# Mamba input products of the first pass in plain float32

## The chip, the cores and the metric

The kernel runs on one core of one Trainium2 chip. The metric is the device time of one execution in microseconds (us), the median over runs; lower is better. The core has a matrix engine (PE, with its weight loads shown apart as PEld), a vector engine (DVE), an activation engine (ACT), GpSimd (POOL), and a queue engine (SP) that here only issues transfers. ACT and POOL issue transfers too. Each engine works through its own list of instructions in order.

## The reference

One layer of a streaming encoder for 512 prompt rows and 8 streams of 16 rows, width 1024, all in float32. What matters here is the front of the layer: the rows are normalized and modulated to `h`, and `h @ w_in` gives ten products. Those of the Mamba branch are `z` (2048 columns) and `xbc` (3072 columns); `xbc` goes through a causal convolution of four taps and a SiLU before the state space scan, and `z` gates the scan's result.

```
h = (_rms(x) * norm1_w * (1.0 + sc1) + sh1).astype(x.dtype)
proj = h @ w_in
q_r, f_r, i_r, g_r, z, xbc, dt_r, ga_r, gb_r = jnp.split(proj, cuts, axis=-1)
...
xc = conv_b + xp[:, 0:t] * conv_w[0]
for j in range(1, SSM_CONV):
    xc = xc + xp[:, j:j + t] * conv_w[j]
xc = jax.nn.silu(xc.astype(f32))
...
y = y.reshape(bn, t, SSM_D_INNER) * jax.nn.silu(z.astype(f32))
```

After the token mixer come the merge of the branches, a product-key lookup and the experts. Results and the final states must agree with a float32 computation.

## The kernel before

The 640 rows are worked on in two passes, with the rows along the free dimension and the features on partitions: pass A (`p`, 256 rows: the first 128 of the prompt and the 128 of the streams) and pass B (`q`, the other 384 rows of the prompt). `run` (line 331) sets the stages in this order: the first modulation of both passes (`first_mod`, line 543); the HGRN inputs of both passes with pass A's HGRN heads (`hgrn_in`, 572); pass A's Mamba (`mamba_in`, 806); pass A's merge and product keys; pass B's HGRN and Mamba with expert rows gathered beside them; pass B's merge and keys; the experts. The kernel is written with a tile framework that orders each engine's instructions itself, by a simulated timeline and with the written order as priority, and adds the waits. So products may stand on PE ahead of work that is written earlier, but every engine's list is fixed when the kernel is built.

A weight block is 1024 x 128 (512 KB), eight chunks of 128 x 128. There are two ways to multiply with it:

- Split (`wsplit` 255, `mm3` 265): SP loads the block to a `raw` buffer (five in this stage); ACT rounds it to `whi` (float32r, line 261) and DVE forms the rest `wlo` (line 253); four buffers of each. The activations lie in SBUF in two parts also, `p.H` (`hhA`, `hlA`). PE then makes three float32r matmuls for each chunk (whi by hlA, whi by hhA, wlo by hhA), 24 for a block, all at line 273. The `raw` buffer is free once DVE has read it.
- Plain (`proj32` 282): SP loads `raw`, and PE multiplies it as float32 with float32 activations, one matmul for each chunk, which the profile shows as two MATMUL records (line 289), so 16 records for a block. The `raw` buffer is free when PE has read it.

`mproj` (292) takes the plain way where the pass has `h32`, the activations kept in float32. Before the change only pass B has it: `first_mod` stores its modulated rows to the DRAM tile `hf_d`, and `run` loads them back after pass A's Mamba (lines 403 and 404).

In `mamba_in`, `mamba_out` (833) runs for four groups. Each takes six convolution products and four z products through `mproj`, so 40 blocks in all; `conv` (772) reads a product from its PSUM bank (ACT `xp`, line 784; DVE `xs`, line 793), and `zproj` (842) by a SiLU on ACT. `mamba_group` (853) then does the scan with float32 matmuls, a chain over ACT, DVE and PE. Between groups stand the 16 gate products (`gate` 827, through `projs` 295), four of them ahead of the first group. Products go to four PSUM banks, `pj`. The tiles of this stage lie in the pools `gtA`, `mcA` and `mpA`, which open where the HGRN pool `gpA` has closed; a new tile waits for those old tiles whose bytes it takes.

Of the kernel before, what the change touches and what calls it, by code (L numbers as in the profile page):

```python
# [8 lines left out]
F32 = mybir.dt.float32  # L9
# [8 lines left out]
P = 128  # L18
D = 1024
KD = D // P  # L20
# [170 lines left out]
class Kernel:  # L191
# [100 lines left out]
    def mproj(self, p, src):  # L292
        return self.proj(src, p.H) if p.h32 is None else self.proj32(src, p.h32)

    def projs(self, src, passes):

        if passes[0].h32 is not None:
            return [self.proj32(src, p.h32) for p in passes]
        w = self.wsplit(src)
        out = []  # L300
        for p in passes:
            ps = self.pj()
            self.mm3(ps, w, P, p.H)
            out.append(ps[:, :p.W])
        self.step()
        return out
# [24 lines left out]
    def run(self):  # L331
        nc, I, V, A, ctx = self.nc, self.I, self.V, self.A, self.ctx
# [28 lines left out]
        p, q = Pass("A", I["xA"], (0, None), 0), Pass("B", I["xB"], (1, 2, 3), 2 * P)  # L361
# [14 lines left out]
        self.wp = hw.enter_context(self.pool("wp"))  # L376
        for t in (p, q):
            t.H = [self.ha.tile([P, KD, t.W], F32R, name="h" + c + t.name) for c in "hl"]
        self.hf_d = self.dram.tile([KD, P, q.W], F32, name="hf_d")
        with self.pool("x1") as xp:  # L380
            self.ada_in(xp)
            ada = self.ada(0)
# [17 lines left out]
        self.nraw, self.nhl = NRAW, NHL  # L400
        bw = ExitStack()
        q.h32 = hb.enter_context(self.pool("hb")).tile([P, KD, q.W], F32, name="h32")
        for j in range(0, KD, 4):
            nc.sync.dma_start(q.h32[:, j:j + 4, :], self.hf_d[j:j + 4].rearrange("m p w -> p m w"))
        self.sr = ctx.enter_context(self.pool("sr", side="right"))
        ah = ExitStack()
        self.rw = ah.enter_context(self.pool("rw", side="right"))
# [3 lines left out]
        sp = bw.enter_context(self.pool("stg"))  # L411
# [131 lines left out]
    def first_mod(self, p, xp):  # L543
        hh, hl = p.H
        for k in range(KD):
            t1 = p.xn[:, k, :]
            self.modulate(p, t1, None, None, self.a1, 0, k)
            if not p.sample:
                self.nc.sync.dma_start(self.hf_d[k], t1)
            self.A.activation(hh[:, k, :], t1, AF.Copy)  # L550
            self.lo(hl[:, k, :], t1, hh[:, k, :])

# [253 lines left out]
    def mamba_in(self, md):  # L806
        nc, I, O, (p, q) = self.nc, self.I, self.O, self.passes
        with self.pool("gtA") as sp:
            p.hist, q.hist = md.tile([P, 24, 8, 3], F32, name="hist"), None
            nc.scalar.dma_start(p.hist, I["hist"])  # L810
            p.cnv, q.cnv = md.tile([P, 24, 8, 3], F32, name="cnvA"), self.md.tile([P, 24, 1, 3], F32, name="cnvB")
            gates = list(range(16))

            def more(n):
                for _ in range(min(n, len(gates))):
                    j = gates.pop(0)
                    self.gate(self.passes if j < GS else self.passes[:1], sp, j)

            more(GA)
            with self.pool("mcA") as p.mc, self.pool("mpA") as mp:  # L820
                for g in range(4):
                    self.mamba_out(p, mp, mp, g)
                    more(GG)
                more(16)
            nc.scalar.dma_start(O["conv_s"], p.cnv)
# [581 lines left out]
```

## Time and profile before

| | |
|---|---|
| median of 3 runs | 2906.17 us (2903.67 to 2910.95) |
| the profiled execution's own time | 2904.54 us |
| its span, first to last instruction | 2902.7 us |
| PE busy | 2697.5 us, 93% of the span |
| DVE busy | 2132.2 us, 73% |
| ACT busy | 1344.4 us, 46% |
| mean granted PE clock | 0.966 of full speed |

Busy time is a union of the records on an engine. A matmul's record is longer than the distance to the next one, because matmuls overlap in the array; what a run of them costs is read from the distance of their starts. "Idle before" a row is time in which the engine had nothing running, with the instruction that ended it. Times within the span are counted from its first instruction.

### The profile page before, as it was taken

The numbers are of one execution on the slowest core, as the hardware profiler recorded it, in microseconds if no ns is written. First come the engines' busy times: TensorE is split into PE (matmuls) and PEld (weight loads), VectorE is DVE, ScalarE is ACT, GpSimd is POOL, SyncE is SP. The second block draws the span as 40 slices with busy tenths as digits, with TensorE's granted clock in tenths as the row PEclk, the third lists the DMA queues.
The fourth block names the chain that finished last, engine by engine and source line by source line (L and its number), as shares of the span: only waits on it lengthen the run. The fifth ranks groups of instructions, "written<-read, shape, count | busy, mean of one in ns | idle before, by whom it ended". The sixth has DMA issues, their size and how long they took to land. (4 is left out here: it accounts for less than half of the span.)

```text
span 2902.7 us, 41739 instructions
## 1 busy us (share of the span) xinstructions
PE 2697.5 (93%) x15177; PEld 2258.9 (78%) x15177; DVE 2132.2 (73%) x4364; ACT 1344.4 (46%) x2056; POOL 731.8 (25%) x682
## 2 busy tenths in 40 slices
PE   6999989998989999977898998997999999999998
PEld 3988868777877555645897777896878999999997
DVE  4556748777778778776788897775667777777776
ACT  3667647764532355644334244554333333333334
POOL 0000002000000443331353476300124444333330
PEclk8999989999999999988998999998999999999999
DMA  8344456657534787666798698967889888888984
GB/s 298 122 150 157 141 181 213 211 175 269 186 115 128 259 293 267 240 218 222 288 330 329 235 338 324 329 224 275 273 285 324 302 313 299 306 302 308 306 303 155
DMA packets 274150, 725.14 MB, mean 250 GB/s; under 512 B 25456, under 2 KB 112760, under 8 KB 270488
## 3 DMA queue, kind: packets, MB, share of 16 engines
q1 hardware_dynamic: 153144, 348.50, 35.7%
q0 software_dynamic: 73920, 269.66, 26.5%
q10 hardware_dynamic: 46880, 104.32, 9.9%
q8 instruction: 119, 1.95, 0.3%
q14 instruction: 87, 0.71, 0.1%
HBM read 646.36 MB, written 76.02 MB: 249 GB/s over the span
## 5 line engine op out<-in xcount | busy, mean ns | idle before, releaser
L1195 POOL DMA_INDIRECT row<-in_u,eidx x256 | 336.5, 1315 | 973.8 <-DVE row L1200 519.8
L1200 DVE SCALAR_TENSOR_TENSOR row<-row,h2t 128x1024 f32<-128x1024 f32 x256 | 307.6, 1220 | 48.1 <-DMA row<-in_u,eidx 47.7
L1294 PE MATMUL po<-vl,wh 128*128 128x512 f32 x768 | 301.0, 392 | 18.8 <-ACT wh L1348 15.2
L289 PE MATMUL pj<-h,raw 128*128 128x384 f32 x896 | 305.2, 495 | 3.2 <-ACT xpB L784 2.3
L1294 PE MATMUL po<-vh,wh 128*128 128x512 f32 x768 | 301.6, 393 | 0.0
L1294 PE MATMUL po<-vh,wl 128*128 128x512 f32 x768 | 299.8, 391 | 0.0
L261 ACT ACTIVATE whi<-raw 128x1024 fp32r<-128x1024 f32 (+1 forms) x169 | 176.5, 1049 | 222.2 <-PE pj L273 135.8
L289 PEld LDWEIGHTS pj<-h,raw 128*128 128x128 f32 x896 | 170.0, 194 | 116.5 <-issue 8.1
L253 DVE TENSOR_TENSOR wlo<-raw,whi 128x1024 fp32r<-128x1024 f32 (+1 forms) x169 | 204.9, 1215 | 63.7 <-ACT whi L261 62.2
L1256 ACT ACTIVATE uh<-ur 128x1024 fp32r<-128x1024 f32 x128 | 135.8, 1061 | 241.9 <-PE s L1264 228.0
L253 DVE TENSOR_TENSOR ul<-ur,uh 128x1024 fp32r<-128x1024 f32 x128 | 156.5, 1222 | 98.7 <-ACT uh L1256 98.5
L1264 PE MATMUL s<-h2h,ul 128*128 128x384 f32 x672 | 225.6, 336 | 0.0
L1264 PE MATMUL s<-h2l,uh 128*128 128x384 f32 x672 | 225.4, 335 | 0.0
L1264 PE MATMUL s<-h2h,uh 128*128 128x384 f32 x672 | 225.1, 335 | 0.0
L1195 POOL DMA_INDIRECT row<-in_v,eidx x128 | 151.2, 1182 | 277.7 <-DVE acc L1210 253.4
L273 PE MATMUL pj<-hlA,whi 128*128 128x256 f32 x648 | 194.0, 299 | 11.2 <-ACT stGA L830 4.9
L273 PE MATMUL pj<-hhA,wlo 128*128 128x256 f32 x648 | 191.4, 295 | 1.6 <-DVE wlo L253 1.6
L273 PE MATMUL pj<-hhA,whi 128*128 128x256 f32 x648 | 191.2, 295 | 0.0
L1294 PEld LDWEIGHTS po<-vl,wh 128*128 128x128 f32 x768 | 145.0, 189 | 49.9 <-ACT wh L1348 15.4
L253 DVE TENSOR_TENSOR vl<-vr,vh 128x1024 fp32r<-128x1024 f32 x128 | 158.5, 1240 | 22.5 <-ACT vh L1306 22.5
L1306 ACT ACTIVATE vh<-vr 128x1024 fp32r<-128x1024 f32 x128 | 135.0, 1056 | 83.7 <-PE po L1294 83.2
L1294 PEld LDWEIGHTS po<-vh,wl 128*128 128x128 f32 x768 | 144.1, 188 | 30.3
(482 smaller groups left out, 7005.6 us busy)
## 6 DMA issues: line engine op xcount, KB each, us to landing
raw<-in_w_in SPq DMA_DIRECT2D x136, 512.0 KB, 4.4
ur<-in_uT SPq DMA_DIRECT2D x128, 512.0 KB, 6.5
vr<-in_vP SPq DMA_DIRECT2D x128, 512.0 KB, 5.8
raw<-in_w_ada SPq DMA_DIRECT2D x48, 512.0 KB, 5.2
g_d<-gt ACTq DMA_DIRECT2D x24, 1024.0 KB, 6.7
gm<-g_d SPq DMA_DIRECT2D x48, 512.0 KB, 7.1
raw<-in_w_b SPq DMA_DIRECT2D x32, 512.0 KB, 5.7
raw<-in_w_q SPq DMA_DIRECT2D x32, 512.0 KB, 4.7
```

The source lines that it names most:

```text
L253: self.V.tensor_tensor(out, raw, hi.bitcast(F32), OP.subtract)
L261: self.A.activation(hi[:, :n], raw[:, :n], AF.Copy)
L273: self.PE.matmul(ps[:m, :W], a[:, k * m:(k + 1) * m], b[:, k0 + k, :], start=start and q == 0, stop=stop and q == 3 * nk - 1)
L289: self.PE.matmul(ps[:, :W], raw[:, k * P:(k + 1) * P], x[:, k, :], start=k == 0, stop=k == KD - 1)
L1195: self.paced(self.G.indirect_dma_start(out=r, out_offset=None, in_=src, in_offset=bass.IndirectOffsetOnAxis(ap=at, axis=0)), pin)
L1200: self.paced(V.scalar_tensor_tensor(r, r, 1.0, self.h2t[:, n, :], OP.mult, OP.mult, accum_out=act[:, s:s + 1]), pin)
L1256: A.activation(uh, ur, AF.Copy)
L1264: PE.matmul(ps[:, :W], a[:, k, :], c[:, k, :], start=q == 0, stop=q == 3 * KD - 1)
L1294: PE.matmul(po[n][hf], a[:, ts], c[:, ds], start=b == 0 and q == 0, stop=b == P - 1 and q == 2)
L1306: A.activation(vh, vr, AF.Copy)
```

## The change

Pass A takes the plain way for its 40 Mamba products too. `first_mod` stores the modulated rows of both passes to DRAM (eight further transfers of 128 KB on SP's queue); `mamba_in` makes a tile `h32` of 8 KB per partition for pass A in `gtA` and loads it with two transfers of 512 KB from SP, written ahead of the first gates. Since `p.h32` is then set, `mproj` takes `proj32` for the convolution and z products, and their weight blocks are no longer split. The gates go through `projs`, whose condition now excludes pass A, so they stay split and `p.H` stays in use.

```diff
+    def h_in(self, p):
+        for j in range(0, KD, 4):
+            self.nc.sync.dma_start(p.h32[:, j:j + 4, :], p.hf_d[j:j + 4].rearrange("m p w -> p m w"))
+
     def projs(self, src, passes):
 
-        if passes[0].h32 is not None:
+        if not passes[0].sample and passes[0].h32 is not None:
             return [self.proj32(src, p.h32) for p in passes]
...
-        self.hf_d = self.dram.tile([KD, P, q.W], F32, name="hf_d")
+        for t in (p, q):
+            t.hf_d = self.dram.tile([KD, P, t.W], F32, name="hf_d" + t.name)
...
-        for j in range(0, KD, 4):
-            nc.sync.dma_start(q.h32[:, j:j + 4, :], self.hf_d[j:j + 4].rearrange("m p w -> p m w"))
+        self.h_in(q)
...
-            if not p.sample:
-                self.nc.sync.dma_start(self.hf_d[k], t1)
+            self.nc.sync.dma_start(p.hf_d[k], t1)
...
+            p.h32 = sp.tile([P, KD, p.W], F32, name="h32", bufs=1)
+            self.h_in(p)
             gates = list(range(16))
```

## Rows read from the trace of the kernel before

**Rows 1.** The page's first part: the busy time of each engine, its share of the span, and its instructions.
```profile
PE 2697.5 (93%) x15177; PEld 2258.9 (78%) x15177; DVE 2132.2 (73%) x4364; ACT 1344.4 (46%) x2056; POOL 731.8 (25%) x682
```

**Rows 2.** The view by stretches: start and end, length, then busy time and records of PE, PEld, DVE, ACT and POOL, mean granted PE clock, DMA share, GB/s. The four stretches are the HGRN inputs, the end of pass A's HGRN, pass A's Mamba up to the last gate product, and the crossing to the merge.
```profile
64.00:366.00 302.00, 301.30 (x2062) 270.00 (x2061) 177.84 (x486) 199.69 (x302) 0.00 (x0) 0.99 0.43 145
366.00:423.40 57.40, 44.29 (x254) 32.60 (x252) 29.41 (x95) 25.07 (x40) 0.64 (x6) 0.83 0.50 167
423.40:657.20 233.80, 217.95 (x1573) 187.76 (x1574) 176.64 (x392) 164.95 (x304) 32.99 (x106) 0.97 0.62 200
657.20:700.00 42.80, 33.82 (x189) 25.55 (x188) 29.78 (x63) 22.18 (x43) 0.00 (x0) 0.88 0.94 335
```

**Rows 3.** The groups of instructions of the stretch from 423.4 to 657.2 us: line, engine, operation, tiles, count, then busy us and mean ns of one, then idle time before and what ended it.
```profile
L273 PE MATMUL pj<-hlA,whi 128*128 128x256 f32 x416 | 126.1, 303 | 11.2 <-ACT stGA L830 4.9 <-DVE xs L793 3.1 <-ACT whi L261 2.2
L273 PE MATMUL pj<-hhA,wlo 128*128 128x256 f32 x416 | 124.2, 298 | 1.6 <-DVE wlo L253 1.6
...
L253 DVE TENSOR_TENSOR wlo<-raw,whi 128x1024 fp32r<-128x1024 f32 x48 | 58.7, 1222 | 13.1 <-ACT whi L261 11.7 <-DMA H<-in_s_ssm 0.7 <-DMA out_ssm_s<-H 0.6
L261 ACT ACTIVATE whi<-raw 128x1024 fp32r<-128x1024 f32 x48 | 50.4, 1052 | 37.6 <-PE pj L273 21.9 <-DMA h_c<-Hs 10.5 <-DMA out_ssm_s<-H 3.4
```

**Rows 4.** PE's timeline in that stage, first and last of a run of 30 split matmuls that nothing interrupts: start, length, line, tiles.
```profile
597.02 0.28 PE L273 MATMUL pj<-hhA,whi 128*128 128x256 f32 x1
...
600.48 0.28 PE L273 MATMUL pj<-hlA,whi 128*128 128x256 f32 x1
```

**Rows 5.** PE's timeline in pass A's product keys, where `proj32` works on the same 256 rows: two whole blocks of 16 records, each with the instruction that follows it.
```profile
822.66 3.62 PE L289 MATMUL pj<-h2f,raw 128*128 128x256 f32 x16
826.12 0.83 PE L672 MATMUL sm<-vh,khat 128*128 128x128 f32 x6
...
831.14 3.62 PE L289 MATMUL pj<-h2f,raw 128*128 128x256 f32 x16
834.60 0.81 PE L319 MATMUL sm<-osq,ones 128*128 128x384 f32 x2
```

**Rows 6.** PE's timeline in pass B, a half block of `proj32` on 384 rows between other float32 matmuls.
```profile
1204.53 2.75 PE L289 MATMUL pj<-h,raw 128*128 128x384 f32 x8
1207.11 0.83 PE L649 MATMUL sm<-lvc 128*128 128x128 f32 x6
```

**Rows 7.** What PE waited for from 423.4 to 657.2 us, longest in total first: who waited, for whom, us in total, times, longest.
```profile
PE sm L327 <- ACT btok L863: 6.0, 2, 3.4
PE pj L273 <- ACT stGA L830: 4.9, 1, 4.9
PE pj L273 <- DVE xs L793: 3.1, 2, 2.3
PE pj L273 <- ACT whi L261: 2.2, 2, 1.1
PE pj L273 <- DVE wlo L253: 1.6, 2, 0.9
PE sm L327 <- DVE cbm L870: 1.0, 1, 1.0
PE sm L319 <- ACT xTg L960: 1.0, 1, 1.0
PE pj L273 <- ACT zt L843: 0.9, 1, 0.9
```

**Rows 8.** PE's timeline at the crossing from HGRN to Mamba: its first product after the wait, and the next.
```profile
423.37 0.58 PE L273 MATMUL pj<-hlA,whi 128*128 128x256 f32 x1 [4.90 <-ACT stGA L830]
423.75 0.41 PE L273 MATMUL pj<-hhA,whi 128*128 128x256 f32 x1
```

**Rows 9.** POOL's timeline there: its first work on a tile of the new pools, with its idle time and what ended it.
```profile
414.61 0.10 POOL L781 MEMSET xpA<- 128x3 f32 x1 [412.04 <-PE sm L690]
```

**Rows 10.** DVE's timeline there: the last instruction of pass A's HGRN.
```profile
420.82 0.42 DVE L708 TENSOR_TENSOR oTA<-oTA,kqA 128x256 f32<-128x256 f32 x1
```

**Rows 11.** DMA throughput from 400 to 445 us in 40 slices of 1.125 us.
```profile
GB/s 222 415 433 408 387 87 4 0 0 0 58 0 0 0 0 0 0 102 189 361 388 353 209 137 117 169 240 388 253 368 257 322 382 233 291 182 106 0 182 366
```

**Rows 12.** DMA issues from 423 to 657 us: tile and source, queue, count, size of one, median us from issue to landing.
```profile
raw<-in_w_in SPq DMA_DIRECT2D x43, 512.0 KB, 4.1
```

**Rows 13.** SP's timeline around the first modulation: start, time for the issues, tile and source, count.
```profile
42.31 0.33 SPq L260 DMA_DIRECT2D raw<-in_w_in  x1
47.51 2.25 SPq L549 DMA_DIRECT2D hf_d<-xB  x4
49.87 0.38 SPq L492 DMA_DIRECT2D raw<-in_w_ada  x1
50.34 2.10 SPq L549 DMA_DIRECT2D hf_d<-xB  x4
```

**Rows 14.** PE's timeline there: the matmuls that wait for that transfer of `w_ada`.
```profile
54.46 1.92 PE L495 MATMUL ad<-raw,cs 128*32 128x512 f32 x4 [3.59 <-DMA raw<-in_w_ada]
```

**Rows 15.** The stores of line 549 (pass B's eight): shortest, median and longest issue in ns, first and last start.
```profile
L549 SPq DMA_DIRECT2D hf_d<-xB x8: 320/416/702, 47.5 to 52.1; - x8
```

## The prediction

> **What bounds the kernel now.** I read the page's first part, then the view by stretches, then in the stage that the change touches its groups, PE's timeline and PE's waits. The first part says that PE is busy 93% of the span and DVE 73% [rows 1]. An average doesn't tell what one stage is worth, so the stage is read alone: pass A's Mamba, from PE's first product after HGRN to its last gate product, is 233.8 us long. PE is busy in 217.95 of them, DVE in 176.64 (76%), ACT in 164.95 (71%) [rows 2]. PE is idle for 15.85 us, and its granted clock is 0.97. Its waits in order of size are for the evacuation of group inputs (ACT `btok`, 6.0), for a free PSUM bank at the very start (4.9, ended by ACT's gate), and for banks that DVE or ACT still reads (`xs` 3.1, `zt` 0.9); for a split weight it waits 2.2 + 1.6 = 3.8 us only [rows 7]. So PE's own work sets the length, and the split on ACT and DVE lies beside it almost entirely. The reader is to see that the change takes work from the two engines that have room and puts some on the one that has none.
>
> A busy PE could still be hollow, since matmul records overlap. The starts settle that: 30 split matmuls with nothing between them start 3.46 us apart from first to last, 0.1193 us each, where each record is 0.28 long [rows 4].
>
> **The change part by part.** *The products.* A split block is 24 matmuls of 0.1193 = 2.863 us [rows 4]. For a plain block on the same 256 rows the trace has the very operation, in the product keys: 16 records, and from their start to the start of what follows 3.46 us, twice over (826.12 - 822.66, 834.60 - 831.14) [rows 5]. Pass B, at 384 rows, agrees: half a block takes 2.58 us, 0.3225 a record, 1.49 times the 0.216 of 256 rows [rows 6]. So a block costs PE 3.46 - 2.863 = 0.60 us more, and 40 blocks 23.9 us. The 12 gates of this stage stay split: 1248 records of line 273 are 52 blocks [rows 3], of which 40 change.
>
> The page "FP8 and Floating Point Precision" of the Trainium skill (section "TensorE Precision Notes") counts true float32 as four passes through the array. Taken against three passes of the split, a plain block would cost 4/3 of 2.863 = 3.82 us, and 40 blocks 38 us. The rows disagree with that ratio: 3.46 / 2.863 is 1.21, because the split's short matmuls don't reach the rate of one pass, so I don't use it in the sum.
>
> *The splits.* 40 times 1.052 us on ACT and 1.222 on DVE go [rows 3], 42 and 49 us in all; four of each lie before 423.4, so 38 and 44 us leave this stage. They are beside PE's work. What they give back is what PE waited for: the 3.8 us for weights, most of which can vanish; and part of the 4.0 us for `xs` and `zt`, where a read of a bank can stand behind a split on DVE or ACT [rows 7]. The 6.0 for `btok` is a chain (product, convolution, SiLU, transpose, copy) that gets a little shorter. Bounds: nothing, and all 15.85 us of idle [rows 2] with the 0.03 of the clock in 233.8 us, 7.0 us more. I take 6 us: 3 of the weights, 2 of the banks, 1 of the chain.
>
> *The buffers.* A `raw` buffer is now held until PE has read it, not until DVE has. Five buffers at 3.46 us make 17.3 us for one turn, against 4.1 us from issue to landing [rows 12]. I cost that at nothing; with bursts of state transfers a landing would have to grow past 13 us to show.
>
> *The load of `h32`.* It is written on SP's queue ahead of the gates' weights, and every weight block stands behind it if the order keeps that. Its bytes were HGRN's. The first touch of a new tile that the trace shows follows a matmul of the last HGRN head, at 414.61 [rows 9]; HGRN's last instruction ends at 420.82 + 0.42 = 421.24 [rows 10]. So the two transfers start between 414.6 and 421.3. DMA is nearly idle from about 407 to 419 us and full from 421 on [rows 11]. With a transfer like the weights', 4.1 us [rows 12], and a second one behind it at some 400 GB/s (1.3 us), `h32` is there between 420.0 and 426.7, later still if it shares with the states' loads. PE's first product starts at 423.37, because a gate must first free a bank [rows 8]. Hence 0 to 3.3 us of new wait, and 2 more with sharing and a PE clock that comes back late: after today's wait the matmul at 423.75 is 0.41 long [rows 8], where the same one takes 0.28 in the steady run [rows 4]. I take 1 us, near the lower end, since `h32` is the first tile of the new pool and the closed pool's first tiles are HGRN's values (`vsb`), which a matmul of line 690 reads last.
>
> *The stores.* Eight more, at 0.416 us each on SP [rows 15]. Pass B's stand from 47.51 to 52.4, and SP issued nothing from 42.64 to 47.51 [rows 13], so pass A's first can fall into that gap. What is queued behind them is the transfer of `w_ada` issued at 49.87; PE waits for it until 54.46 [rows 14] and has no slack afterwards, as the HGRN stretch is PE-bound without a gap (301.30 of 302.00) [rows 2]. Bounds 0 and 8 x 0.416 = 3.3 us; I take 1, as some four of eight come before it and part of those fall into the gap. The reverse, a gain, is excluded: nothing is taken from that queue.
>
> *Afterwards.* The crossing to the merge waits on the scan's tail and on transfers, with PE busy 33.82 of 42.80 [rows 2]; its instructions don't change. Everything after pass A's Mamba moves as a whole. The order on all engines is made anew, which can move any stage by a few us either way; I give that 5 us in the range and nothing in the sum.
>
> **Sum:** 23.9 - 6 + 1 + 1 = +19.9 us. On the profiled execution (2904.54, of which 2902.7 are span) that is 2924.4; the median of the runs lies 1.6 above that execution, so 2926.
>
> **The rivals.**
>
> *1. The freed engines pay for it (not slower).* With ACT and DVE down to 54% and 57% of its old length, (165 - 38) / 234 and (177 - 44) / 234, no wait is left and the clock stays up: 15.85 + 7.0 = 22.9 us come back against 25.9 (23.9 + 2 of transfers). That gives +3, 2909. It speaks for it that more filler on PE hides chains; against it that only 3.8 us of the waits name a split, and that the 4.9 at the start and the first gates have nothing to do with one. It decides in favour of "no change" once more than 17 us come back.
>
> *2. Faster.* The end of pass A's HGRN has 13.1 us of idle PE and a clock of 0.83 [rows 2]. If the planner put the first products there, up to 13.1 + 0.17 x 57.4 = 22.9 us could go: 2926 - 23 = 2903, and with the 17 us that rival 1 has beyond my 6, 2886. Against it: products need a PSUM bank, which the four gates hold until 423, and `h32`, whose bytes are HGRN's until 414.6.
>
> *3. `h32` comes late.* SP waits for HGRN's last instruction, the weights wait behind it, and PE restarts at about 430 at half its clock: 5 to 9 us beyond my 1, so 2931 to 2935.
>
> *4. The plain block is dearer here than in the product keys.* At 4/3 of the split's time (3.82 us) the products cost 38.2 us and the sum is 34, 2940. Against it are two blocks measured at 3.46 and pass B's rate. The Trainium skill's four passes, above, would make it so; the trace doesn't bear that out.
>
> That the change doesn't do what it says can't be: `p.h32` is set before `mproj` is first called.
>
> **How the numbers follow.** The forecast, 2918 to 2934 by the bounds of the waits and transfers: 0.60. Rival 1: 0.15. Rival 2: 0.04. Rival 3: 0.17. Rival 4 with an unlucky new order: 0.04. A measurement here can tell about 0.3%, 8.7 us: slower means over 2914.9, faster under 2897.5. Rival 3, rival 4 and the forecast lie above, with a little of rival 1: 0.82. Rival 1's rest and half of rival 2 are "same": 0.15. Faster 0.03. The range leaves out the outer parts of rivals 1, 2 and 4: 2908 to 2940.
>
> **What would show it.** Line 289 with 320 plain matmuls more, as 640 records, pitch 0.216 us; line 273 with 960 fewer; 40 instructions fewer each of lines 261 and 253. The stretch from PE's first Mamba product to the last gate should be about 252 us instead of 233.8, with PE as busy as now or more and ACT and DVE at 50 to 55%. If it is under 240 us, the waits were worth more than I gave (rival 1). If PE sits idle beyond 423 for a DMA of `h32`, rival 3 is right. If the stage is as forecast and the whole isn't, the new order of a later stage did it. I would be wrong on the main term if plain blocks in this stage start closer than 3.4 us apart.

## The result, and the profile after

The changed kernel takes 2921.9 us (median of 5 runs, 2918.17 to 2932.4) against 2906.17: a ratio of 1.0057 over all runs (the two medians alone give 1.0054), interval 1.0036 to 1.0078. A second set of runs of the same source (e2 below) gives 1.004 (1.0022 to 1.0058). So it is slower by 12 to 16 us. The forecast was 2926, with 2908 to 2940 as its range. The profiled execution of after takes 2920.55 us, of which 2918.8 are its span.

Lines behind the added method stand 4 further down in after, from `first_mod` on 3, and from `mamba_in`'s load on 5; lines 253 to 289 keep their numbers. First the page's first part, which answers to [rows 1]:

```profile
PE 2721.4 (93%) x14857; PEld 2260.0 (77%) x14857; DVE 2091.1 (72%) x4324; ACT 1320.0 (45%) x2024; POOL 718.2 (25%) x682
```

PE has 23.9 us more work with 320 records fewer (960 float32r matmuls went, 640 plain records came). DVE has 40 instructions fewer and ACT, on balance, 32. PE's growth in this row is the main term of the prediction (23.9) almost to the digit, but a busy sum isn't a path, and in the stage itself PE's busy time grows by 20.4 us. The path is read by stretches; the same four as in [rows 2], with the boundaries where after has them:

```profile
64.80:366.80 302.00, 301.51 (x2052) 268.18 (x2052) 178.00 (x486) 199.92 (x303) 0.31 (x2) 0.99 0.44 146
366.80:416.43 49.63, 39.51 (x248) 27.68 (x246) 24.00 (x88) 20.95 (x35) 0.41 (x4) 0.96 0.52 176
416.43:659.75 243.32, 238.32 (x1258) 189.03 (x1258) 141.42 (x361) 144.06 (x276) 21.68 (x106) 0.99 0.59 200
659.75:702.50 42.75, 31.53 (x162) 23.02 (x162) 26.84 (x58) 22.05 (x42) 0.00 (x0) 0.88 0.93 324
```

Row by row against [rows 2]: the HGRN inputs are as long as before and 0.8 later; the end of HGRN is 49.6 us instead of 57.4; the Mamba stage is 243.3 instead of 233.8; the crossing has the same length, but its records are 162 instead of 189, so less is done in it. In the Mamba stage PE is idle for 243.32 - 238.32 = 5.00 us instead of 15.85, and its granted clock is 0.99 instead of 0.97.

What PE still waited for in that stage, the answer to [rows 7]:

```profile
PE pj L289 <- ACT stGA L835: 5.3, 1, 5.3
PE sm L331 <- ACT btok L868: 3.9, 3, 1.8
PE pj L289 <- DVE xs L796: 0.7, 2, 0.5
```

The first row is the wait ahead of the stage's first product and so not in its length. The waits for split weights (3.8 us before) are gone, and the five others of [rows 7] that lie inside the stage have shrunk from 12.0 us to 4.6.

PE's timeline there, 80 plain records in a row and what follows them, shows the price of a plain block in its new place, as [rows 5] did for the product keys:

```profile
437.09 17.43 PE L289 MATMUL pj<-h,raw 128*128 128x256 f32 x80
454.36 0.38 PE L331 MATMUL sm<-con,bct 128*128 128x128 f32 x2
```

454.36 - 437.09 = 17.27 us for five blocks: 3.454 us a block, 0.2159 a record. The forecast had 3.46.

Since the span grows at several places, here is where, from first and last starts of the same lines in two profiled executions of each kernel (the second ones are the experiments e1 and e2 below):

| us from the span's start | before | before again | after | after again | mean change |
|---|---|---|---|---|---|
| PE's first Mamba product | 423.4 | 420.3 | 416.4 | 414.5 | -6.4 |
| from it to the last gate product | 233.4 | 230.4 | 243.0 | 245.5 | +12.3 |
| from there to the first product key | 165.9 | 165.5 | 169.4 | 171.8 | +4.9 |
| from there to the experts' first product | 815.2 | 812.2 | 817.0 | 818.2 | +3.9 |
| from there to the experts' last | 1253.4 | 1264.5 | 1262.1 | 1266.1 | +5.1 |

The last row says little: the two executions of the kernel before lie 11 us apart there by themselves. The four rows above it add up to +14.7 us, and agree with the 12 to 16 us of the timed runs. (With the last row it is 19.8: e1's profiled execution is among the fastest of its runs and e2's is the slowest of its own.)

### The profile page after: what moved, and what is told of

It reads as the page before. It is cut to its first block, busy times and chain, and to the rows that moved or that the text cites. A ratio compares the mean times of both kernels' runs of the same rounds, so it can differ in the third digit from the quotient of the medians.

```text
span 2918.8 us, 41028 instructions
## 1 busy us (share of the span) xinstructions
PE 2721.4 (93%) x14857; PEld 2260.0 (77%) x14857; DVE 2091.1 (72%) x4324; ACT 1320.0 (45%) x2024; POOL 718.2 (25%) x682
## 5 line engine op out<-in xcount | busy, mean ns | idle before, releaser
L289 PE MATMUL pj<-h,raw 128*128 128x384 f32 (+1 forms) x1536 | 451.6, 449 | 9.6 <-ACT stGA L835 5.3
L289 PEld LDWEIGHTS pj<-h,raw 128*128 128x128 f32 x1536 | 291.6, 193 | 148.3 <-issue 15.7
L1299 PE MATMUL po<-vl,wh 128*128 128x512 f32 x768 | 300.7, 392 | 17.9 <-ACT wh L1353 14.7
L253 DVE TENSOR_TENSOR ul<-ur,uh 128x1024 fp32r<-128x1024 f32 x128 | 156.4, 1222 | 107.3 <-ACT uh L1261 99.1
L261 ACT ACTIVATE whi<-raw 128x1024 fp32r<-128x1024 f32 (+1 forms) x129 | 134.6, 1048 | 175.7 <-PE pj L273 118.2
L253 DVE TENSOR_TENSOR wlo<-raw,whi 128x1024 fp32r<-128x1024 f32 (+1 forms) x129 | 155.7, 1212 | 53.2 <-ACT whi L261 50.9
L1299 PEld LDWEIGHTS po<-vl,wh 128*128 128x128 f32 x768 | 144.7, 188 | 49.6 <-ACT wh L1353 14.9
L1299 PEld LDWEIGHTS po<-vh,wh 128*128 128x128 f32 x768 | 144.7, 188 | 28.4
L1215 DVE SCALAR_TENSOR_TENSOR acc<-row,act,acc 128x1024 f32<-128x1024 f32 x127 | 162.3, 1278 | 0.9
L1353 ACT ACTIVATE wh<-w 128x384 fp32r<-128x384 f32 x119 | 62.4, 525 | 204.7 <-DVE w L1352 189.8
```

Of the source, the lines that this page charges most:

```text
L253: self.V.tensor_tensor(out, raw, hi.bitcast(F32), OP.subtract)
L261: self.A.activation(hi[:, :n], raw[:, :n], AF.Copy)
L289: self.PE.matmul(ps[:, :W], raw[:, k * P:(k + 1) * P], x[:, k, :], start=k == 0, stop=k == KD - 1)
L1215: self.paced(V.scalar_tensor_tensor(acc, r, w, acc, OP.mult, OP.add), pin)
L1299: PE.matmul(po[n][hf], a[:, ts], c[:, ds], start=b == 0 and q == 0, stop=b == P - 1 and q == 2)
L1353: A.activation(wh, w, AF.Copy)
```

## The experiments

The theory: PE's dearer products are the price (+24 in the stage), the freed engines give part of it back, and what is left in the table is due to the new order and repeats. Against it: the differences away from the Mamba stage are variation of single executions; the relief is small and something else makes the stage shorter than 252; or the cost lies in the transfers. All runs are timed in five rounds against the kernel before on the same chip.

**e1 and e2: each kernel once more.** No edit, a copy of before and a copy of after.

> The kernel before, once more, to see which differences between two profiles repeat. Theory A (each kernel's fixed order sets its stages): ratio 1.000, first Mamba product of pass A at 423 us within 2, last gate product at 657 within 2, merge's first yl product at 707, first expert product of the last stage (h2l,uh into s) at 2011 within 3. Theory B (the differences outside pass A's Mamba are variation between executions): some of these places move by 5 us or more.

> The changed kernel, once more. Theory A: 2922 within 5, ratio 1.0055; first Mamba product at 416, last gate product at 659, first yl product at 718, first expert product into s at 2028, each within 3. Theory B: the start of Mamba lies between 416 and 423, or the growth after 660 us (8 us in the merge, 9 us in the experts' first part) is gone or elsewhere.

e1: 2913.94 us, 1.001 (0.9992 to 1.0027). e2: 2925.16, 1.004 (1.0022 to 1.0058). The stretches of the Mamba stage, of e1 and then of e2:

```profile
420.30:651.00 230.70, 216.32 (x1573) 186.12 (x1574) 176.55 (x392) 164.99 (x303) 32.68 (x106) 0.98 0.64 203
```

```profile
414.50:660.30 245.80, 238.06 (x1258) 188.67 (x1258) 141.47 (x361) 144.17 (x276) 21.81 (x106) 0.99 0.60 197
```

The early start, the longer stage and the longer way to the product keys repeat. The experts don't: their first part (up to the last product with `U`) takes 338.8 and 346.4 us in two executions of the kernel before, and 347.8 and 347.7 in after, so most of the 9 us that the first pair of profiles shows there is variation. Over all fourteen profiles of this study that part takes 338 to 349 us, and e11, a changed kernel, has 339.5.

**e3 and e5: the relief without the dearer products.** Both are the kernel before, whose 40 blocks are loaded but not split; the 40 products multiply with one block that was split once. In e3 the fixed parts take 8 KB of `gtA`, in e5 one part stands for both and lies in a pool of its own on the other side, so that no tile of the stage moves.

```diff
...
+        raw = self.wp.tile([P, 1024], F32, name="raw", bufs=self.nraw)
+        self.nc.sync.dma_start(raw, src.rearrange("p k c -> p (k c)"))
+        ps = self.pj()
+        self.mm3(ps, (self.wfix, self.wfix), P, p.H)      # e3: self.wfix, a pair
...
+            hi, lo = self.wsplit(I["w_in"][40])
+            wf = ExitStack()
+            self.wfix = wf.enter_context(self.pool("wf", side="right")).tile([P, 1024], F32R, name="wf")
+            A.activation(self.wfix, hi.bitcast(F32), AF.Copy)
```

> The kernel before, but the 40 Mamba products of pass A are all taken with one block that is split once, so 24 float32r matmuls a product stay on PE and the 40 splits on ACT and DVE are gone; the 40 weight blocks are still loaded and not used, so the products are not those of the reference. Theory A (the freed engines give back about 15 us, 11 of idle PE and 4 of clock): Mamba from first product to last gate about 219 us instead of 233.8, the whole 2885 to 2897. Theory C (as forecast, they give back 6 and the rest of the gain came from PE having more work to put in the gaps): stage about 228, the whole about 2900.

> The relief alone again, with the once-split block in a place where it moves no other tile: 24 float32r matmuls a product from one block (both parts of it are the rounded half), no splits for the 40 products, their weights loaded and not used, so the products are not the reference's. In e3 a wait of 13.7 us for a bank, behind transfers on ACT's queue, hid what the stage gained. Theory A (relief worth about 15 us in the stage): from PE's first Mamba product to the last gate product 214 to 222 us, the whole 0.4 to 0.6% faster, ratio 0.994 to 0.996. Theory C (6 us): stage 226 to 229, ratio 0.998.

e3: 2913.49, 0.9998 (0.9981 to 1.0016). e5: 2905.03, 0.9998 (0.9983 to 1.0013). The longest wait of PE in e3's stage, and then e5's stage and its longest wait:

```profile
PE pj L273 <- DVE xs L799: 14.5, 2, 13.7
```

```profile
419.10:645.50 226.40, 213.01 (x1574) 183.66 (x1574) 136.64 (x355) 132.55 (x267) 21.54 (x106) 0.97 0.54 184
```

```profile
PE pj L273 <- DVE xs L799: 11.9, 2, 10.5
```

Both edits bring a wait of their own that neither kernel has, of 13.7 us and of 10.5, so e3 decides nothing and e5 gives a bound: with that wait in it the stage is 226.4 us, against a mean of 232.2 for before. The relief alone is worth 6 us, as the 6 of the forecast would have it, and if the one long wait is taken off, some 16. None of it reaches the end: the time is that of the kernel before. The way from the last gate to the merge's first product with `yl` is 55.9 us in e5 and 50.3 in before, and from the product keys to the experts 820 and 814: what the stage saves is given back there.

**e4: the changed kernel with its splits kept.** The 40 blocks are rounded and subtracted as before, and nothing reads the two parts.

```diff
...
+        if split:
+            hi = self.wp.tile([P, 1024], F32R, name="whi", bufs=self.nhl)
+            lo = self.wp.tile([P, 1024], F32R, name="wlo", bufs=self.nhl)
+            self.A.activation(hi, raw, AF.Copy)
+            self.lo(lo, raw, hi)
...
```

> The changed kernel, but ACT and DVE still split the 40 blocks and nobody uses the parts: PE's cost without the relief. Theory A: Mamba about 255 us long (233.8 + 23.9 - 3), 9 to 14 us longer than in the changed kernel, the whole 2930 or more. Theory C: about 246, within 4 us of the changed kernel.

2941.72 us, 1.0106 (1.0084 to 1.0129); 16.6 us over e2 on the same chip. Its stage, and PE's longest waits in it:

```profile
423.40:683.30 259.90, 243.39 (x1258) 192.34 (x1258) 179.46 (x396) 181.77 (x313) 33.86 (x106) 0.97 0.57 187
```

```profile
PE sm L336 <- ACT btok L873: 7.9, 3, 3.8
PE sm L328 <- ACT xTg L970: 5.8, 3, 2.5
PE pj L294 <- ACT stGA L840: 5.6, 1, 5.6
```

This is the cleanest reading of the study. The stage with the dearer products and without the relief is 259.9 us, more than either theory gave it: 26 more than the 233.8 of [rows 2], where the prediction had 23.9 for the products and 1 for the load of `h32`. Without the splits it is 243.3 and 245.8, a mean of 244.6: taking them away is worth 15.3 us in this stage. The waits say how: `btok` and `xTg` are ends of chains over ACT and DVE, and splits stand in front of them in those engines' lists. The trace of before has such a place. ACT makes two splits ahead of `btok`, and PE waits 2.51 us for it (ACT's timeline, then PE's):

```profile
522.38 2.00 ACT L261 ACTIVATE whi<-raw 128x1024 fp32r<-128x1024 f32 x2
...
524.54 0.39 ACT L863 ACTIVATE btok<-sm 128x256 f32<-128x256 f32 x1
```

```profile
524.99 0.44 PE L327 MATMUL sm<-con,xTg 128*128 128x128 f32 x2 [2.51 <-ACT btok L863]
```

The early start is gone here too (423.4); why is read with e11.

**e6: the transfers without the plain products.** The changed kernel stores and loads `h32`, and `mproj` still splits for pass A.

```diff
     def mproj(self, p, src):
-        return self.proj(src, p.H) if p.h32 is None else self.proj32(src, p.h32)
+        return self.proj(src, p.H) if p.sample else self.proj32(src, p.h32)
```

> The changed kernel with the eight stores, the tile h32 and its two loads, but the products still taken from the split weights as before (the loaded h32 is not used): the transfers and the new order without PE's cost and without the relief. As forecast: +2 us, ratio 1.000 to 1.001, the stage 230 to 234. If the transfers or the tile that shifts the others cost the 5 us that the changed kernel loses between the last gate product and the product keys, that stretch is 170 us here too, not 166.

2916.37 us, 1.0033 (1.0018 to 1.0047). Its stage:

```profile
422.30:659.50 237.20, 220.38 (x1571) 189.78 (x1572) 176.77 (x391) 167.12 (x305) 29.03 (x106) 0.95 0.64 201
```

Ten transfers that nothing needs cost 9 us, where the forecast had 2. The stage is 5 us longer than the mean of before at a lower clock, the way to the product keys is that of before (166.0), and the way from there to the experts 13 us longer (827.1). Nothing reads `h32` of pass A here, so nothing waits for its landing. What is left are the place that the transfers take on SP's queue and in the DMA engines, and another order on every engine that the scheduler makes around them; this run can't part the one from the other. The run serves for something else as well: e4 has the same transfers and makes the same splits, and differs in what PE multiplies. Its stage is 259.9 - 237.2 = 22.7 us longer, with PE idle for about as long (16.5 and 16.8 us). So 22.7 is the price of the 40 plain blocks by themselves, forecast 23.9.

**e9: PE's work in the stage enlarged.** The changed kernel with ten chunks in each of the 40 products, the last two of them taken a second time: 40 x 4 records x 0.216 = 34.6 us more for PE and nothing more for anything else.

```diff
...
+        ks = list(range(KD)) + ([6, 7] if more else [])
+        for n, k in enumerate(ks):
+            self.PE.matmul(ps[:, :W], raw[:, k * P:(k + 1) * P], x[:, k, :], start=n == 0, stop=n == len(ks) - 1)
```

> The changed kernel with ten chunks to each of the 40 products instead of eight (the last two chunks are taken twice, so the products are not the reference's): PE gets 40 x 4 records of 0.216 us more, 34.6 us, and no other engine anything. If PE sets the stage's length, Mamba goes from 244 to 274 to 279 us and the whole 28 to 36 us past the changed kernel, ratio to the kernel before about 1.016. If the chain over ACT and DVE sets it, the stage grows by less than 20.

2947.1 us, 1.0129 (1.011 to 1.0148). Its stage:

```profile
414.80:690.30 275.50, 272.13 (x1418) 219.56 (x1418) 143.65 (x361) 126.14 (x261) 20.26 (x106) 0.99 0.54 176
```

The stage grows by 275.5 - 244.6 = 30.9 us for 34.6 of PE's work, and PE is idle in 3.4 of it: it is PE that sets this stage. The whole grows by less than the 28 to 36 us expected, 2947.1 - 2921.9 = 25, or 22 against e2.

**e7 and e11: why the stage starts earlier in after.** The conditioning products (`ada`, line 495 in before) are issued by `step`. Both kernels call it once more behind each HGRN head, e7 in before and e11 in after, so that those products are done sooner.

```diff
                     self.hgrn_head(p, ta, h, kq, vh)
+                    self.step()
```

> The kernel before, but the conditioning products (w_ada) run one step ahead more for each HGRN head of pass A, so that they are done before the last heads. If the changed kernel's gain of 5 to 7 us at the end of HGRN comes from w_ada landing later than its matmuls are due there, with PE's clock falling in the wait, pass A's Mamba starts at 413 to 417 here and the whole is 0.1 to 0.3% faster. If it comes from the split weights having left ACT and DVE, it starts at 420 to 423 as before.

> The changed kernel with the conditioning products run ahead, as in e7. If its gain of 6 us at the end of HGRN comes from conditioning matmuls that stand between the last head's steps and hold PE's clock up, taking them away there loses it: Mamba starts at 421 to 427 instead of 415, the granted clock from 405 to 415 us is 0.5, and the whole is 4 to 10 us slower than the changed kernel. If not, it starts at 413 to 417.

e7: 2916.6, 1.0025 (1.001 to 1.0041). e11: 2928.15, 1.0078 (1.0061 to 1.0095). Both are slower, against what I expected of e7, whose stage starts at 426.4. The clock shows a part of why. The view by stretches of 5 us at the end of HGRN (the last three columns are clock, DMA share and GB/s), of before, after and e11:

```profile
395.00:400.00 5.00, 2.28 (x12) 0.96 (x10) 3.45 (x7) 2.40 (x3) 0.00 (x0) 1.00 1.03 315
400.00:405.00 5.00, 2.41 (x8) 1.85 (x8) 4.12 (x18) 2.95 (x5) 0.00 (x0) 0.51 0.94 373
405.00:410.00 5.00, 4.22 (x16) 3.58 (x17) 2.86 (x11) 0.80 (x2) 0.00 (x0) 0.50 0.18 67
410.00:415.00 5.00, 5.00 (x23) 4.63 (x22) 0.29 (x1) 0.43 (x2) 0.37 (x4) 0.50 0.04 13
```

```profile
400.00:405.00 5.00, 3.68 (x18) 1.76 (x14) 3.09 (x12) 0.98 (x3) 0.00 (x0) 0.82 0.42 135
405.00:410.00 5.00, 4.76 (x29) 3.28 (x30) 0.45 (x2) 0.97 (x3) 0.00 (x0) 1.00 0.34 118
```

```profile
400.00:405.00 5.00, 3.06 (x14) 2.64 (x14) 3.69 (x16) 1.24 (x3) 0.00 (x0) 0.55 0.08 28
405.00:410.00 5.00, 4.53 (x22) 4.13 (x21) 0.74 (x2) 0.38 (x1) 0.00 (x0) 0.50 0.04 13
410.00:415.00 5.00, 5.00 (x14) 3.11 (x15) 1.42 (x6) 2.08 (x3) 0.00 (x0) 0.59 0.00 0
```

In before PE is busy for 2.28 of the 5 us from 395, and the next 15 are granted 0.50, which is 1.2 GHz. In after the clock is back at 1.00 (2.4 GHz) from 405 to 415. PE's timelines of before, after and e11 show what that does to the last head:

```profile
398.81 1.05 PE L495 MATMUL ad<-raw,cs 128*32 128x512 f32 x4 [2.23 <-DMA raw<-in_w_ada]
...
410.03 3.43 PE L686 MATMUL sm<-qtA,S0A 128*128 128x16 f32 x16
...
414.29 3.30 PE L698 MATMUL sm<-veA,khatA 128*128 128x512 f32 x4
```

```profile
399.66 1.92 PE L499 MATMUL ad<-raw,cs 128*32 128x512 f32 x4
...
405.24 1.05 PE L499 MATMUL ad<-raw,cs 128*32 128x512 f32 x4 [1.00 <-DMA raw<-in_w_ada]
...
406.55 1.86 PE L689 MATMUL sm<-qtA,S0A 128*128 128x16 f32 x16
...
408.78 1.88 PE L701 MATMUL sm<-veA,khatA 128*128 128x512 f32 x4
```

```profile
407.17 3.44 PE L690 MATMUL sm<-qtA,S0A 128*128 128x16 f32 x16
...
422.65 7.52 PE L289 MATMUL pj<-h,raw 128*128 128x256 f32 x22 [7.12 <-DMA h<-hf_dA]
```

In after two groups of conditioning products happen to lie between the head's small matmuls, one of them as late as 405.24, and the head's 16 state products take 1.86 us instead of 3.43. In e11, where those products come sooner, they take 3.44 again and the early start is gone. e11 shows a form of rival 3 as well: SP issues the load of `h32` at 415.98, behind a weight transfer that waited for a conditioning product, and PE waits 7.12 us. Most of that wait would have been there without the load, since ACT frees the bank only then:

```profile
419.99 0.66 ACT L836 ACTIVATE stGA<-pj 128x256 f32<-128x256 f32 x2
```

The first of these two ends near 420.4, against 416.4 in after; so of the 7.2 us by which e11's stage starts later than the mean of after, some 5 belong to the end of HGRN and some 2 to `h32`.

The place of the conditioning products isn't the whole cause, though. In e4 one group of them stands even at 404.58, and the clock is at 0.50 from 405 to 415 all the same. e4 differs from after in the splits alone, and DVE's timeline shows two of them between the small instructions (`lvcA` and others) that PE's matmuls of the last head wait for:

```profile
399.51 1.22 DVE L253 TENSOR_TENSOR wlo<-raw,whi 128x1024 fp32r<-128x1024 f32 x1
...
402.72 1.22 DVE L253 TENSOR_TENSOR wlo<-raw,whi 128x1024 fp32r<-128x1024 f32 x1
```

PE is busy for 2.21 of the 5 us from 400 there, against 3.68 in after. No profile of a kernel that still splits all 40 blocks, or 24 of them as e10 does, starts the stage before 420 us (before, e1, e4, e6, e7, e8, e10, e12: 420.3 to 426.4). Of the six without these splits, after, e2 and e9 start at 414.5 to 416.4, and e3, e5 and e11, each of which places other work differently, at 419.1 to 424.8. So the 6.4 us at the start come with the freed engines, a relief outside the stage that the prediction didn't look for, and a small difference of order can lose them again.

**e8: the subtraction on POOL.** The kernel before, `wlo` of the 40 blocks on POOL instead of DVE. It asks whether the relief of DVE alone could be had without dearer products.

```diff
...
+        (lo_on or self.V).tensor_tensor(lo[:, :n], raw[:, :n], hi[:, :n].bitcast(F32), OP.subtract)
```

> The kernel before, but the subtraction of the split (wlo) of the 40 products is done by POOL instead of DVE; rounding stays on ACT, PE keeps its 24 matmuls. If DVE's share of the relief is the larger part of it and POOL is fast enough (40 subtractions in 234 us), the stage is 220 to 228 us and the whole 0.2 to 0.4% faster, faster than both kernels. If POOL needs more than about 4 us for one, PE waits for wlo and the stage grows past 240.

2928.68 us, 1.0078 (1.0057 to 1.0099). POOL's group and the stage:

```profile
L262 POOL TENSOR_TENSOR wlo<-raw,whi 128x1024 fp32r<-128x1024 f32 x36 | 87.5, 2438 | 38.5 <-ACT whi L261 37.9 <-ACT xpA L784 0.4
```

```profile
421.00:677.20 256.20, 225.89 (x1573) 190.43 (x1574) 196.66 (x358) 167.77 (x305) 112.63 (x142) 0.94 0.57 182
```

One takes 2438 ns there against 1222 on DVE [rows 3], the stage is 24 us longer than the mean of before, and DVE isn't freed: it is busy for 196.66 us, 20 more than in [rows 2], though 36 subtractions (44 us) are gone. The expectation had asked whether POOL needs more than 4 us for one; at 2.4 the stage grows all the same, with PE waiting 18.0 us for DVE's `xw` and `xs` and 4.6 for POOL's `wlo`. DVE's other work has become slower, as two of its groups show, in e8 and then in before (busy us and mean ns of one behind the bar):

```profile
L788 DVE SCALAR_TENSOR_TENSOR caccA<-xpA,cols,caccA 128x128 f32<-128x128 f32 x72 | 43.0, 607 | 11.7 <-ACT caccA L786 11.4
...
L951 DVE TENSOR_SCALAR bm<-btok,con 128x128 f32<-128x128 f32 x26 | 16.1, 630 | 0.0
```

```profile
L788 DVE SCALAR_TENSOR_TENSOR caccA<-xpA,cols,caccA 128x128 f32<-128x128 f32 x72 | 24.6, 347 | 22.8 <-ACT caccA L786 22.6
...
L951 DVE TENSOR_SCALAR bm<-btok,con 128x128 f32<-128x128 f32 x26 | 7.1, 281 | 0.0
```

The same instructions take 607 ns for 347 and 630 for 281. One of them in e8, and POOL's subtraction beside it, from the two timelines:

```profile
499.98 2.18 DVE L788 SCALAR_TENSOR_TENSOR caccA<-xpA,cols,caccA 128x128 f32<-128x128 f32 x1 [0.58 <-ACT caccA L786]
```

```profile
499.64 2.36 POOL L262 TENSOR_TENSOR wlo<-raw,whi 128x1024 fp32r<-128x1024 f32 x1 [0.63 <-ACT whi L261]
```

DVE's instruction ends 0.16 us after POOL's. The page "SBUF — State Buffer" of the Trainium skill (section "SBUF: two separate sides") says that DVE and GpSimd share one pair of SBUF ports, and that a GpSimd instruction, or a DVE instruction of certain kinds (a two-port mode, or two inputs in SBUF), holds it until it ends, so that the other engine blocks. These rows fit that, but no run here isolates it, and not every group grew (line 954, 684 and 685 ns).

**e10 and e12: a better point between or beside?** e10 is the changed kernel with only the 16 z products plain. e12 is the kernel before with two gates ahead of the first group instead of four.

```diff
-            self.conv(p, mp, cb, self.mproj(p, self.I["w_in"][40 + cb]), dst)
+            self.conv(p, mp, cb, self.proj(self.I["w_in"][40 + cb], p.H) if p.sample else self.mproj(p, self.I["w_in"][40 + cb]), dst)
```

```diff
-GA = 4
+GA = 2
```

> The changed kernel with only the 16 z products in plain float32 and the 24 convolution products split. PE's cost by the forecast's price is 16 x 0.597 = 9.6 us, and 16 of 40 splits leave ACT and DVE. If relief and cost go in proportion, the stage is 232 + 0.4 x 12 = 237 and the ratio 1.002; if the first splits that go give the most relief, the stage is 228 to 234 and the kernel as fast as before or faster.

> The kernel before with two gate products ahead of the first Mamba group instead of four (GA = 2), all products split. With four, the gates hold the four banks from about 380 us until ACT reads them at 423, and PE's clock is at half in that wait. If work on PE at the end of HGRN is what keeps the clock up there, the first convolution products run before 415 us, the granted clock between 405 and 415 is over 0.7, and Mamba's last gate product comes 5 to 10 us earlier: ratio 0.996 to 0.998, faster than both kernels. If the banks or the order don't let them through, it starts at 420 to 423 and the ratio is 0.999 to 1.004, as the other changes of order have given.

e10: 2923.87, 1.0055 (1.0035 to 1.0075). e12: 2917.83, 1.0038 (1.0023 to 1.0053). e10's stage and its longest wait, and e12's stage:

```profile
422.50:666.70 244.20, 230.01 (x1446) 190.74 (x1446) 162.44 (x378) 161.12 (x294) 25.73 (x106) 0.95 0.60 196
```

```profile
PE sm L323 <- ACT xTg L965: 12.3, 3, 4.3
```

```profile
423.90:664.30 240.40, 222.79 (x1574) 192.17 (x1575) 180.58 (x398) 168.56 (x306) 26.66 (x106) 0.94 0.62 195
```

Neither is better, and e10 misses both of its expectations. e10 has 16 / 40 of PE's extra work (9.6 us) and the whole time of after: its stage is as long as after's, with a wait of 12.3 us for `xTg` that after doesn't have and a clock of 0.95. e12 starts the stage at 423.9, so fewer gates ahead of it bring no early start. Of the kernels that compute the layer, the one before stays the fastest.

## Why the prediction was right, and where it was right by luck

**The main term held.** PE sets the stage (e9: 30.9 of 34.6 us), a plain block there costs 3.454 us where 3.46 was forecast, and with the relief kept out the stage grows by 26 us (e4), of which 22.7 are the products by e4 against e6; forecast 23.9. The 3.82 us that the prediction estimated from the four passes of the page "FP8 and Floating Point Precision" of the Trainium skill (section "TensorE Precision Notes") don't agree with the 3.454 measured; rival 4 falls with them. That estimate took the split's time for a matmul as the time of one pass, so its failure doesn't show the number of passes to be wrong.

**The relief was mis-sized.** The step that failed is "I take 6 us: 3 of the weights, 2 of the banks, 1 of the chain". By the stretches, PE's idle time in the stage fell by 15.85 - 5.00 = 10.85 us, and of the clock 0.03 x 233.8 = 7.0 became 0.01 x 243.3 = 2.4, another 4.6 (an estimate: the clock is read to 0.01, which is 2.3 us here). Together that is 15.4; with it the stage comes to 233.8 + 23.9 - 15.4 = 242.3, measured 243.3; e4 against after says 15.3 by another way. By the waits, the weights gave all of their 3.8, the banks 3.3 of 4.0, the chain of `btok` 2.1, and `cbm` and `xTg`, which the sum didn't have, 2.0. The prediction's own bound (nothing to 22.9) held it; the point from which rival 1 decides, 17 us, was nearly reached. The mistake was to give only 3 us to the 12.0 us of waits that don't name a split, and nothing to the clock. A wait names the last instruction before the release; the splits stood in the same engines' lists ahead of those, as at 522.38.

**Outside the stage the relief gives and takes.** The prediction gave the new order 5 us in the range and nothing in the sum. Two of the three differences that it was to cover go with the splits rather than with the order as such. The 6.4 us at HGRN's end are one (e4 and e11 above); rival 2 had seen that up to 22.9 us lay there, though it looked to products placed earlier. The 4.9 us on the way to the product keys are the other: that way takes 164.8 to 166.5 us in the eight profiles of kernels that split, whose orders differ, and 167.0 to 173.4 in the six that don't. So a part of what the stage gains is lost again there. The view by stretches of that way, of before and then of after, shows no new work:

```profile
656.80:822.66 165.86, 146.25 (x1074) 133.26 (x1072) 128.22 (x305) 86.34 (x145) 0.00 (x0) 0.96 0.61 205
```

```profile
659.40:828.80 169.40, 147.77 (x1071) 135.66 (x1070) 127.56 (x303) 86.62 (x145) 0.00 (x0) 0.94 0.60 201
```

PE is busy 1.5 us longer at a lower clock (0.94 for 0.96) and idle 2.0 us longer, with as many records. Which chain holds it up there isn't shown. Three kernels that change hardly anything but the order or what moves it are slower too: e6 by 0.33%, e7 by 0.25%, e12 by 0.38%. That the order causes the 3.9 us between the keys and the experts is argued from these, not shown: no wait there was traced to it.

**The small terms.** The eight stores: the HGRN inputs end 0.8 us later in the first pair of profiles and 0.3 in the second, forecast 1. The load of `h32`, forecast 1: SP issued it at 408.98, PE's first product waited for the gate alone, so 0 in after. That this came near the forecast was luck of a kind, as e11's wait shows. And stores and load together, with the order that they bring, cost 9 us of the whole in e6, where the sum had 2.

**So the sum** 23.9 - 6 + 1 + 1 = 19.9 meets a measured 12 to 16 because errors cancel in part. The record has the change step by step, each against the kernel before: the transfers alone 1.0033 (e6), with the plain products 1.0106 (e4), and with the splits gone 1.0040 to 1.0057 (e2 and after). In us these steps are about +10, +21 and -14 to -19, where the sum had +2, +23.9 and -6; by the intervals of the runs each is uncertain by up to 8. The sign and the range rest on the main term, which was sound; the closeness doesn't. "About 252 us" for the stage was 6 to 9 too high, and at 243.3 to 245.8 it missed the mark of 240, below which the text would have seen rival 1.

**What stays open.** Whether the 9 us of e6 are the transfers or the order. How large the relief is where nothing else changes: 6 us in e5 with a wait of its own in it, 15 beside dearer products. How much of the early start needs the conditioning products where after has them. And why savings in this stage are lost before the experts (e5).

## What to carry to other kernels

Where one engine sets a stage, moving work from idle engines onto it costs its full price, but count the relief from all idle time and clock that the stage has, not mainly from waits that name the removed instruction: here 15 us, not 6. Look for it in the stages beside it too, where the removed instructions also stood. Price the operation from a place in the same trace where it already runs: 3.46 us was right to 0.01, an estimate by passes was off by 11%. Build the change step by step, as e6, e4 and after do, and each term of the sum has a run of its own. And when a scheduler writes the order anew, give the order a share of its own (here 0.25 to 0.4% for edits that should cost nothing), and profile each kernel twice before a difference in a late stage is read as an effect.

## What the runs showed of the hardware

- The last head of HGRN runs at a granted clock of 0.50 in before, and the same 16 matmuls take 3.43 us there and 1.86 in after at 1.00. With the splits kept beside it (e4), or with the conditioning products moved away (e11), the clock is 0.50 again.
- The split's 24 float32r matmuls of 256 columns take 2.863 us and eight plain float32 ones 3.454, a ratio of 1.21 for the same block.
- A subtraction of 128 x 1024 in float32 takes 2438 ns on POOL and 1222 on DVE, and while POOL makes it some of DVE's own instructions stretch, one kind from a mean of 347 to 607 ns, another from 281 to 630 (e8).
- One and the same kernel, on one chip, takes 2899.3 to 2923.9 us (26 runs of before beside e1 to e4), a spread larger than the effect that was measured.
